# One stock of eight weight tiles in the FFN, and a shorter combination, in a two-layer attention, mLSTM and SwiGLU trunk

## The chip, the cores and the metric

The kernel runs on one core of one Trainium2 chip, as one launch. The metric is the device time of one execution in microseconds; the time before is the median of three runs. The engines are TensorE (PE; PEld where it loads weights), VectorE (DVE), ScalarE (ACT), GpSimd (POOL) and SyncE (SP), which issues nearly all loads.

## What is computed

Two layers on x of 256 rows and 2048 columns, all in float32. A layer normalizes, mixes (layer 0: sliding-window attention beside an mLSTM; layer 1: forgetting attention), adds, normalizes, and runs the FFN with 5632 hidden columns:

```python
def swiglu(xn, w_gate, w_up, w_down):
    return (jax.nn.silu(xn @ w_gate) * (xn @ w_up)) @ w_down

for layer in range(DEPTH):            # DEPTH = 2
    xn = rms_norm(h, norm_mix[layer])
    mix = swa_mlstm_mixer(...) if layer % 2 == 0 else forgetting_attention_mixer(...)
    h = h + mix
    h = h + swiglu(rms_norm(h, norm_ffn[layer]), w_gate[layer], w_up[layer], w_down[layer])
return rms_norm(h, norm_final)
```

## The kernel before

**Precision by splitting.** Every float32 operand of a large product is split in two: `hi`, cast by ScalarE to the reduced type float32r, and `lo`, the remainder, made by VectorE as the operand minus `hi`. A product is then three matmuls, hi by hi, hi by lo and lo by hi (`three`, L509 to L511, and the same in `gemm`, L212 to L214). x is kept as `xh`, `xl` and the input of the second product of each stage as `mh`, `ml`, both as 16 blocks of 128 rows (k) by 256 tokens; the tokens make two halves of 128, t0 and t1.

**Plain and mixed blocks.** `pair_group` multiplies by two weight matrices at once (gate and up; or two column blocks of w_down), 512 columns of each. It walks over pairs of k blocks in the order of `ORDER` (or `DOWN`): an entry (0, pair) is a plain block, (1, pair) a mixed one. A plain block loads 2 x 512 KB, splits both pieces and runs 2 x 2 x 2 x 3 = 24 matmuls into four PSUM banks, `plain`. A mixed block trades one product of eight for additions, in the manner of Strassen and Winograd: VectorE forms four sums of the two weight pieces (L568 to L571), these are split too (`ht`, `lt`), and they multiply sums of the x blocks that were formed once a layer (`sums_of`, kept in `sx`; for the down products in `sd`). It runs 21 matmuls, part into `plain` and part into four further banks, `prods`. At the end of the group `combine` (L523 to L530) forms from the four products the four corrections `c`, and these are added to `plain` (L619) before Silu (L621) and the product of gate and up (L623). A down group adds `c` and then `plain` into h (L708, L353).

**The FFN's course.** 11 groups of gate and up per layer, in parts of 3, 4 and 4 (`PARTS`). After each part its hidden columns are turned (by DMA transposes, or on TensorE after a last group) into `mh`, `ml`, and w_down's rows of that part are multiplied in two groups of 2 x 512 columns; the last half of the last layer uses `gemm` instead. The first FFN group takes over the turning of the second half of x: `todo` holds the joins that are due after the third and the fifth position (`LATER`), each of which splits a quarter of x and forms the sums of the mixed pairs 1, 3 and 5 in it.

**Tiles.** Weight pieces land in `raw` tiles, four in pool `wr` for plain blocks and four in the layer's pool `fp` for mixed ones. Their splits go to pool `wp`: tags `hi` and `lo`, six buffers each, taken in turn (L174, L175; for a mixed block also L565, L566). The two splits of a mixed block's sums go to tags `ht` and `lt` in `fp`, two buffers each (L578, L579). A tile is written again once the last matmul that reads it is done.

**What sets the order.** The program is written once, in the order of the Python code; a scheduler then lays the instructions of all engines out along its own timeline and fixes each engine's list. `issue_after` and the due times only steer it. Each engine runs its list in order and waits on counters of the other engines.

Of the kernel before, what the change touches and what calls it, by code (L numbers as in the profile page):

```python
# [24 lines left out]
CK = 2  # L25
# [10 lines left out]
ORDER = ((0, 0), (1, 1), (0, 2), (1, 3), (0, 4), (1, 5), (0, 6), (0, 7))  # L36
DOWN = {
# [35 lines left out]
def trunk(  # L73
# [26 lines left out]
    wp = ctx.enter_context(tc.tile_pool(name="wp", bufs=6))  # L100
# [72 lines left out]
    def split_chunk(raw, n):  # L173
        hi = wp.tile([P, CK, NB], F32R, tag="hi", name="hi")  # L174
        lo = wp.tile([P, CK, NB], F32R, tag="lo", name="lo")  # L175
        for k in (slice(0, 1), slice(1, CK)) if any(raw is f for f in fine) else (slice(0, CK),):
            latest[0] = nc.scalar.copy(hi[:, k, 0:n], raw[:, k, 0:n])  # L177
            nc.vector.tensor_tensor(  # L178
                out=lo[:, k, 0:n], in0=raw[:, k, 0:n], in1=hi[:, k, 0:n].bitcast(F32), op=ALU.subtract
            )  # L180
        return hi, lo
# [71 lines left out]
    def sums_of(pool, sh, sl, copies, full=None, tags=("tmp", "tmp"), bufs=None, box=None):  # L253
# [239 lines left out]
    def out_proj(w, idx, key, extra):  # L493
        last, rest = KT - 4, []
        for n0 in (0, 2):
# [3 lines left out]
            for i in range(2):  # L499
                gemm(accs[i], m_of, w, (n0 + i) * NB, NB, last, KT, KT, step=6)  # L500
                add_out(accs[i], n0 + i)
                (later if n0 == 0 else rest).append(
                    (LATER[n0 + i], split_turned(idx, n0 + i, *scrap(extra[2], n0 + i), extra))
                )
                square_sum(key, n0 + i)
        return rest

# [8 lines left out]
    def pair_group(fp, par, lhs, sums, mats, order, todo=(), halves=None, inner=None, raws=None):  # L516
        plain = [[bank(par, "acc") for _ in range(NT)] for _ in range(2)]
        todo = list(todo)
# [13 lines left out]
        for pos, (kind, pair) in enumerate(order):  # L532
# [4 lines left out]
            if not kind:  # L537
# [4 lines left out]
                for m, (w, c0) in enumerate(mats):  # L542
                    hi, lo = load_chunk(w, k0, c0, NB)
                    run_due(todo, pos)
                    for i, t in walk:
# [4 lines left out]
                            pos == 0 and i == 0, last and i == CK - 1,  # L550
# [14 lines left out]
            hu = wp.tile([P, CK, NB], F32R, tag="hi", name="hi")  # L565
            lu = wp.tile([P, CK, NB], F32R, tag="lo", name="lo")  # L566
# [6 lines left out]
            for src in (ra, rb) if halves else (t4, ra):  # L573
# [15 lines left out]
            three(plain[0][0], xb[:, t0], lb[:, t0], hg[:, 1, :], lg[:, 1, :], False, False)  # L589
            three(plain[1][0], sh[:, 3, :], sl[:, 3, :], hu[:, 1, :], lu[:, 1, :], False, False)  # L590
            three(prods[1], sh[:, 0, :], sl[:, 0, :], ht[0], lt[0], first, last)
            three(prods[2], sh[:, 2, :], sl[:, 2, :], ht[1], lt[1], first, last)
            three(prods[3], sh[:, 1, :], sl[:, 1, :], ht[2], lt[2], first, last)
            three(plain[0][1], xb[:, t1], lb[:, t1], ht[3], lt[3], False, False)
# [4 lines left out]
    def ffn(layer, fp, sx, sd, key, todo, idx_next=None, key_next=None, finish=None):  # L599
        r = rstd(key)  # L600

        def sums_x(pair):
            j = mixed_of(ORDER).index(pair)
            return sx[0][:, j, :, :], sx[1][:, j, :, :]

        for g0, g1 in zip(PARTS, PARTS[1:]):
# [3 lines left out]
            for g in range(g0, g1):  # L610
                par = (g1 - 1 - g) % 2
                plain, c = pair_group(
                    fp, par, x_of, sums_x, [(w_gate[layer], g * NB), (w_up[layer], g * NB)], ORDER, todo
                )
                todo = []
                for m in range(2):
                    for t in range(NT):
                        o = c[:, 2 * m + t, :]
                        nc.vector.tensor_tensor(out=o, in0=plain[m][t], in1=o, op=ALU.add)  # L619
                for t in range(NT):  # L620
                    nc.scalar.activation(c[:, t, :], c[:, t, :], AF.Silu, scale=r[:, t : t + 1])  # L621
                for t in range(NT):
                    nc.vector.scalar_tensor_tensor(  # L623
                        out=c[:, t, :], in0=c[:, 2 + t, :], scalar=r[:, t : t + 1], in1=c[:, t, :], op0=ALU.mult, op1=ALU.mult
# [47 lines left out]
            def sums_d(pair, order=order):  # L672
                j = mixed_of(order).index(pair)
                return sd[0][:, j, :, :], sd[1][:, j, :, :]
# [16 lines left out]
            for n0 in (0, 2):  # L691
# [13 lines left out]
                for m in range(2):  # L705
                    for t in range(NT):
                        o = h[:, t, (n0 + m) * NB : (n0 + m + 1) * NB]
                        nc.vector.tensor_tensor(out=o, in0=c[:, 2 * m + t, :], in1=o, op=ALU.add)  # L708
# [3 lines left out]
    def close_layer(layer, w_out, idx, key, **rest):  # L712
        with tc.tile_pool(name=f"fp{layer}", bufs=2) as fp:
# [3 lines left out]
            todo = out_proj(w_out, idx, key, (*sx, fp))  # L717
            sd = [fp.tile([P, nd, 4, P], F32R, tag=f"sd{i}", name=f"sd{i}", bufs=1) for i in range(2)]
            ffn(layer, fp, sx, sd, key, todo, **rest)
# [3 lines left out]
    hi = wp.tile([P, CK, NB], F32R, tag="hi", name="hi")  # L723
    lo = wp.tile([P, CK, NB], F32R, tag="lo", name="lo")
# [17 lines left out]
    with tc.tile_pool(name="ev", bufs=1) as ev:  # L742
# [223 lines left out]
        with tc.tile_pool(name="mp", bufs=1) as mp:  # L966
            def sums_m(pair):
                j = mixed_of(MIXQ).index(pair)
                return sx[0][:, j, :, :], sx[1][:, j, :, :]
# [129 lines left out]
    with tc.tile_pool(name="od", bufs=1) as od:  # L1099
# [65 lines left out]
        def sums_x(pair):  # L1165
            j = mixed_of(MIX).index(pair)
            return sx[0][:, j, :, :], sx[1][:, j, :, :]
# [154 lines left out]
```

## Time and profile before

| | us |
|---|---|
| median of three runs (lowest to highest) | 2077.54 (2077.33 to 2078.0) |
| span of the profiled execution | 2076.6 |
| TensorE busy (share of the span) | 2066.4 (100%) |
| VectorE busy | 1824.5 (88%) |
| ScalarE busy | 1374.7 (66%) |
| bytes read from HBM | 408.68 MB, 198 GB/s over the span |

The profiled execution's own time is its span; the median of the runs stands 0.9 us above it. A matmul's end in the profile is modelled and overlaps the start of the next, so a busy TensorE alone doesn't say that it runs at its full pace: the distance from start to start does. Busy times of VectorE and ScalarE are unions of overlapping instructions. The layout of the run: layer 0's mixer until about 323 us, its FFN until about 1010, layer 1's mixer until about 1380, its FFN until the end.

### The profile page before, as it was taken

To read this page: it belongs to the slowest core of one execution; us is meant where nothing else is said; L and a number is where in the kernel's file an instruction comes from. 1 tells how busy PE (TensorE), PEld (TensorE's weight loads), DVE (VectorE), ACT (ScalarE), POOL (GpSimd) and SP (SyncE) were. 2 spreads that over 40 slices of the span, in tenths; PEclk is the share of its full clock that TensorE was granted. 3 is DMA by queue.
4 is the path that set the end of the run, shared out by engine and by line. 5 is a ranking of instruction groups with operands and counts; after the bars stand their busy time and mean duration, and the time that the engine had idled before them with its cause. 6 is when DMAs were issued, how large, how long until landed. Compare 5 with 4: busy or idle time off the path is not lost.

```text
span 2076.6 us, 26994 instructions
## 1 busy us (share of the span) xinstructions
PE 2066.4 (100%) x9473; PEld 1715.0 (83%) x9473; DVE 1824.5 (88%) x2410; ACT 1374.7 (66%) x1736; POOL 41.7 (2%) x66
## 2 busy tenths in 40 slices
PE   9999999999999999999999999999999999999998
PEld 7878888888888888888888888888888888888887
DVE  6788769999999999999899778689999999999994
ACT  6777678765676656667676776687655667456763
POOL 1010000000000000000000001000000000000000
PEclk9999999999999999999999999999999999999999
DMA  8566577666566666666576866586665667666764
GB/s 292 172 213 188 190 247 236 203 217 206 189 230 223 205 210 205 220 212 204 185 215 204 235 193 184 156 283 220 206 205 200 213 206 234 203 202 213 220 197 138
DMA packets 309575, 434.87 MB, mean 209 GB/s; under 512 B 106412, under 2 KB 114624, under 8 KB 309312
## 3 DMA queue, kind: packets, MB, share of 16 engines
q1 hardware_dynamic: 307088, 426.27, 65.1%
q0 software_dynamic: 1632, 5.80, 0.8%
q8 instruction: 74, 1.21, 0.2%
q10 hardware_dynamic: 720, 1.09, 0.2%
q14 instruction: 61, 0.50, 0.1%
HBM read 408.68 MB, written 2.12 MB: 198 GB/s over the span
## 4 chain that ended last, share of the span: by engine, by line
PE 97%; DVE 1%; ACT 1%; DMA 1%; issue 1%; SPq 0%; POOLq 0%; POOL 0%; ACTq 0%; DVEq 0%
PE acc L510 21%; PE acc L509 21%; PE acc L511 21%; PE acc L213 5%; PE acc L212 5%; PE acc L214 5%; PE prod L509 5%; PE prod L510 5%; PE prod L511 5%; PE p L369 1%; PE po L470 1%; DMA raw<-in_w_in_odd_dram 0%; ACT s L403 0%; PE po L471 0%; DVE lo L178 0%
## 5 line engine op out<-in xcount | busy, mean ns | idle before, releaser
L177 ACT CAST hi<-raw 128x1024 fp32r<-128x1024 f32 (+3 forms) x656 | 664.8, 1028 | 440.2 <-PE acc L511 269.1
L178 DVE TENSOR_TENSOR lo<-raw,hi 128x1024 fp32r<-128x1024 f32 (+3 forms) x656 | 772.8, 1192 | 146.3 <-ACT hi L177 143.5
L510 PE MATMUL acc<-lo,xh 128*128 128x512 f32 x1254 | 488.6, 390 | 0.0
L509 PE MATMUL acc<-hi,xh 128*128 128x512 f32 x1254 | 485.9, 390 | 0.5 <-ACT hi L177 0.5
L511 PE MATMUL acc<-hi,xl 128*128 128x512 f32 x1254 | 484.8, 389 | 0.0
L510 PEld LDWEIGHTS acc<-lo,xh 128*128 128x128 f32 x1254 | 235.4, 188 | 49.4 <-DVE lo L178 0.6
L509 PEld LDWEIGHTS acc<-hi,xh 128*128 128x128 f32 x1254 | 235.2, 188 | 49.5 <-ACT hi L177 0.7
L511 PEld LDWEIGHTS acc<-hi,xl 128*128 128x128 f32 x1254 | 235.4, 188 | 48.8
L510 PE MATMUL acc<-lo,mh 128*128 128x512 f32 x437 | 169.7, 389 | 0.0
L511 PE MATMUL acc<-hi,ml 128*128 128x512 f32 x437 | 168.4, 389 | 0.0
L509 PE MATMUL acc<-hi,mh 128*128 128x512 f32 x437 | 167.9, 389 | 0.0
L339 ACT CAST hi<-raw 128x512 fp32r<-128x512 f32 x109 | 67.6, 620 | 89.4 <-PE acc L511 80.5
L213 PE MATMUL acc<-lo,mh 128*128 128x512 f32 (+1 forms) x322 | 126.3, 392 | 0.0
L212 PE MATMUL acc<-hi,mh 128*128 128x512 f32 (+1 forms) x322 | 125.8, 391 | 0.0
L214 PE MATMUL acc<-hi,ml 128*128 128x512 f32 (+1 forms) x322 | 123.7, 391 | 0.0
L340 DVE TENSOR_TENSOR lt<-t,ht 128x1024 fp32r<-128x1024 f32 x95 | 115.8, 1219 | 5.2 <-ACT ht L339 5.1
L339 ACT CAST ht<-t 128x1024 fp32r<-128x1024 f32 x95 | 99.9, 1051 | 30.7 <-PE prod L511 28.8
L339 ACT CAST ht<-raw 128x1024 fp32r<-128x1024 f32 x95 | 99.7, 1050 | 29.7 <-PE acc L511 15.0
L340 DVE TENSOR_TENSOR lt<-raw,ht 128x1024 fp32r<-128x1024 f32 x95 | 115.7, 1218 | 1.8 <-ACT ht L339 1.8
L213 PE MATMUL acc<-lo,xh 128*128 128x512 f32 (+3 forms) x288 | 99.8, 348 | 0.2 <-DVE lo L178 0.2
L214 PE MATMUL acc<-hi,xl 128*128 128x512 f32 (+3 forms) x288 | 98.1, 344 | 0.0
L212 PE MATMUL acc<-hi,xh 128*128 128x512 f32 (+3 forms) x288 | 95.9, 347 | 0.3
(363 smaller groups left out, 3448.0 us busy)
## 6 DMA issues: line engine op xcount, KB each, us to landing
raw<-in_w_gate_dram SPq DMA_DIRECT2D x176, 512.0 KB, 4.5
raw<-in_w_up_dram SPq DMA_DIRECT2D x176, 512.0 KB, 4.6
raw<-in_w_down_dram SPq DMA_DIRECT2D x176, 512.0 KB, 5.1
raw<-in_w_in_odd_dram SPq DMA_DIRECT2D x88, 512.0 KB, 4.9
raw<-in_w_in_even_dram SPq DMA_DIRECT2D x51, 512.0 KB, 5.0
raw<-in_w_out_even_dram SPq DMA_DIRECT2D x32, 512.0 KB, 5.1
raw<-in_w_out_odd_dram SPq DMA_DIRECT2D x32, 512.0 KB, 4.8
hr<-in_w_in_even_dram SPq DMA_DIRECT2D x12, 512.0 KB, 4.6
```

Source lines behind the costliest of these rows:

```text
L177: latest[0] = nc.scalar.copy(hi[:, k, 0:n], raw[:, k, 0:n])
L178: nc.vector.tensor_tensor(out=lo[:, k, 0:n], in0=raw[:, k, 0:n], in1=hi[:, k, 0:n].bitcast(F32), op=ALU.subtract)
L212: nc.tensor.matmul(o, ah[:, ts], hi, start=(k == 0), stop=False)
L213: nc.tensor.matmul(o, ah[:, ts], lo, start=False, stop=False)
L214: nc.tensor.matmul(o, al[:, ts], hi, start=False, stop=(k == k_all - 1 and cs.stop == n))
L339: nc.scalar.copy(dst_h, src)
L340: nc.vector.tensor_tensor(out=dst_l, in0=src, in1=dst_h.bitcast(F32), op=ALU.subtract)
L369: nc.tensor.matmul(pq[j % 2][:, j // 2, :], q_of(j, b), k_of(j)[:, 0:cols], start=True, stop=True)
L470: nc.tensor.matmul(po, v_of(j, 0), tt[:, j, 0:2, :].rearrange("p c q -> p (c q)"), start=True, stop=False)
L509: nc.tensor.matmul(o, ah, hi, start=start, stop=False)
L510: nc.tensor.matmul(o, ah, lo, start=False, stop=False)
L511: nc.tensor.matmul(o, al, hi, start=False, stop=stop)
```

## The change

The six slots of `wp` become a list of six pairs of fixed tiles, `weights`. `slot()` hands them out in turn, to plain blocks, to mixed blocks' raw pieces and, in the FFN, to the splits of their sums. In each layer's `close_layer` (output projection and FFN) two more pairs join the list and leave it at the end; they take the room of the `ht` and `lt` buffers in `fp`. In the mixers the splits of the sums go elsewhere (`halves`), as before. `combine`, where it belongs to the FFN, lays `c` out with the token half first and makes the last two adds one, whose first operand is one product read twice by a repeated access. The adds of `c` into h take 1024 columns at a time. `HEAVY` is an order with four mixed blocks; `DENSE`, the set of groups that would use it, is empty. The sums that the fourth pair (`FOURTH = 7`) would need are formed all the same: three of the four in places of `xh`, `xl` that ORDER leaves unread (`rooms`), the fourth in a new tile, `x4`. The scratch space of GpSimd's DMAs is halved from 4096 to 2048. `fresh` marks the first matmul into a bank; with ORDER it gives what the condition before it gave.

```diff
+HEAVY = ((1, 1), (0, 0), (1, 3), (0, 2), (1, 5), (0, 4), (1, 7), (0, 6))
+FOURTH = 7
+DENSE = ()
...
-    wp = ctx.enter_context(tc.tile_pool(name="wp", bufs=6))
+    wp = ctx.enter_context(tc.tile_pool(name="wp", bufs=1))
+    weights = [[wp.tile([P, CK, NB], F32R, name=f"{a}{i}") for a in ("hi", "lo")] for i in range(6)]
+
+    def slot():
+        weights.append(weights.pop(0))
+        return weights[-1]
...
     def split_chunk(raw, n):
-        hi = wp.tile([P, CK, NB], F32R, tag="hi", name="hi")
-        lo = wp.tile([P, CK, NB], F32R, tag="lo", name="lo")
+        hi, lo = slot()
...
-        split_plain(sh, sl, s)
+        if x4 is None:
+            split_plain(sh, sl, s)
+        else:
+            split_plain(sh, sl, s[:, 0:3, :])
+            split_plain(x4[:, 0, :], x4[:, 1, :], s[:, 3, :])
...
-            if extra is not None and pair in mixed_of(ORDER):
-                sh, sl, pool = extra
-                j = mixed_of(ORDER).index(pair)
+            if extra is not None and (pair in mixed_of(ORDER) or pair == FOURTH):
+                sh, sl, x4, pool = extra
...
-                sums_of(pool, sh[:, j, :, :], sl[:, j, :, :], copies)
+                if pair == FOURTH:
+                    sums_of(pool, rooms(xh), rooms(xl), copies, x4=x4)
+                else:
+                    j = mixed_of(ORDER).index(pair)
+                    sums_of(pool, sh[:, j, :, :], sl[:, j, :, :], copies)
...
+    def rooms(m):
+        return m[:, 2:11:4, P:S]
...
             c = fp.tile([P, 4, NB], F32, tag="c", name="c", bufs=1)
             nc.scalar.copy(c[:, 0, :], prods[0])
+            if halves is None:
+                nc.vector.tensor_tensor(out=c[:, 1, :], in0=prods[3], in1=c[:, 0, :], op=ALU.add)
+                nc.vector.tensor_tensor(out=c[:, 2, :], in0=prods[2], in1=c[:, 1, :], op=ALU.add)
+                nc.vector.tensor_tensor(
+                    out=c[:, 1:4:2, :],
+                    in0=prods[1].rearrange("p (a n) -> p a n", a=1).broadcast_to([P, 2, NB]),
+                    in1=c[:, 1:3, :],
+                    op=ALU.add,
+                )
+                return c
...
-            hu = wp.tile([P, CK, NB], F32R, tag="hi", name="hi")
-            lu = wp.tile([P, CK, NB], F32R, tag="lo", name="lo")
+            hu, lu = slot()
...
-                    hs = fp.tile([P, 2, NB], F32R, tag="ht", name="ht")
-                    ls = fp.tile([P, 2, NB], F32R, tag="lt", name="lt")
+                    hs, ls = slot()
...
-                for m in range(2):
-                    for t in range(NT):
-                        o = h[:, t, (n0 + m) * NB : (n0 + m + 1) * NB]
-                        nc.vector.tensor_tensor(out=o, in0=c[:, 2 * m + t, :], in1=o, op=ALU.add)
+                for t in range(NT):
+                    o = h[:, t, n0 * NB : (n0 + 2) * NB]
+                    nc.vector.tensor_tensor(
+                        out=o, in0=c[:, 2 * t : 2 * t + 2, :].rearrange("p a n -> p (a n)"), in1=o, op=ALU.add
+                    )
...
             sx = [fp.tile([P, nx, 4, P], F32R, name=f"sx{i}", bufs=1) for i in range(2)]
-            todo = out_proj(w_out, idx, key, (*sx, fp))
+            x4 = fp.tile([P, 2, P], F32R, name="x4", bufs=1)
+            more = [[fp.tile([P, CK, NB], F32R, name=f"{a}{i}", bufs=1) for a in ("hi", "lo")] for i in (6, 7)]
+            weights.extend(more)
+            todo = out_proj(w_out, idx, key, (*sx, x4, fp))
...
+            for pair in more:
+                weights.remove(pair)
...
-    nc = _bacc.Bacc("TRN2", target_bir_lowering=False, num_devices=1, dynamic_dma_scratch_size=4096)
+    nc = _bacc.Bacc("TRN2", target_bir_lowering=False, num_devices=1, dynamic_dma_scratch_size=2048)
```

More of the change, by code (lines that the diff above doesn't have):

```diff
@@ L251, in whole, with sums_of @@
         )
[L253 removed]
+    def sums_of(pool, sh, sl, copies, full=None, tags=("tmp", "tmp"), bufs=None, box=None, x4=None):
         if box is not None:
@@ L506, in out_proj, with four @@
         return rest
+    def four(s, j):
+        return [s[:, j, e, :] for e in range(4)]
+    def rooms(m):
+        return m[:, 2:11:4, P:S]
     def three(o, ah, al, hi, lo, start, stop):
@@ L517, in pair_group, with fresh @@
         plain = [[bank(par, "acc") for _ in range(NT)] for _ in range(2)]
+        begun = set()
+        def fresh(*at):
+            known = at in begun
+            begun.add(at)
+            return not known
         todo = list(todo)
@@ L588, in pair_group @@
             three(prods[0], xa[:, t0], la[:, t0], hg[:, 0, :], lg[:, 0, :], first, last)
[L589 to L594, printed above, removed]
+            three(plain[0][0], xb[:, t0], lb[:, t0], hg[:, 1, :], lg[:, 1, :], fresh(0, 0), False)
+            three(plain[1][0], sh[3], sl[3], hu[:, 1, :], lu[:, 1, :], fresh(1, 0), False)
+            three(prods[1], sh[0], sl[0], ht[0], lt[0], first, last)
+            three(prods[2], sh[2], sl[2], ht[1], lt[1], first, last)
+            three(prods[3], sh[1], sl[1], ht[2], lt[2], first, last)
+            three(plain[0][1], xb[:, t1], lb[:, t1], ht[3], lt[3], fresh(0, 1), False)
         if inner is None:
@@ L612, in ffn @@
                 plain, c = pair_group(
-                    fp, par, x_of, sums_x, [(w_gate[layer], g * NB), (w_up[layer], g * NB)], ORDER, todo
+                    fp,
+                    par,
+                    x_of,
+                    sums_x,
+                    [(w_gate[layer], g * NB), (w_up[layer], g * NB)],
+                    HEAVY if g in DENSE else ORDER,
+                    todo,
                 )
```

32 lines of the change are left out of this document (19 added, 13 removed).

## The prediction

> **What bounds the kernel now.** I read the page's head first, then TensorE's own list of waits, then the busy time by stretches of steady and unsteady stages, and last the timelines that show how far VectorE runs ahead of TensorE. The page of the kernel before:
>
> ```profile
> span 2076.6 us, 26994 instructions
> ...
> PE 2066.4 (100%) x9473; PEld 1715.0 (83%) x9473; DVE 1824.5 (88%) x2410; ACT 1374.7 (66%) x1736; POOL 41.7 (2%) x66
> ...
> PE 97%; DVE 1%; ACT 1%; DMA 1%; issue 1%; SPq 0%; POOLq 0%; POOL 0%; ACTq 0%; DVEq 0%
> ```
>
> TensorE is busy for 2066.4 of 2076.6 us and carries 97% of the chain. Its waits (total, times, longest, us) are these and no others:
>
> ```profile
> PE cold L159 <- POOL ones L156: 1.2, 1, 1.2
> PE acc L509 <- ACT hi L177: 0.5, 1, 0.5
> PE acc L213 <- DVE lo L178: 0.2, 1, 0.2
> ```
>
> 1.2 us lies before the first matmul. The other two, 0.7 us, are all that TensorE visibly lost to late operands in two layers. A modelled matmul end can hide a short slip, so the pace must be looked at too. Stretches, with busy time and count of PE, PEld, DVE, ACT, POOL, then clock and DMA:
>
> ```profile
> 323.00:364.30 41.30, 41.30 (x184) 34.21 (x183) 38.62 (x54) 35.95 (x50) 0.69 (x1) 1.00 0.74 228
> 841.10:882.60 41.50, 41.50 (x185) 34.35 (x183) 39.78 (x51) 28.36 (x32) 0.00 (x0) 1.00 0.66 216
> 1020.00:1120.00 100.00, 99.50 (x460) 82.74 (x459) 90.72 (x119) 69.98 (x83) 4.15 (x5) 1.00 0.74 230
> ```
>
> 841.10 to 882.60 is one gate/up group: five plain blocks of 24 matmuls and three mixed ones of 21, so 183, in 41.5 us: 0.227 us each, with VectorE 96% busy (39.78 of 41.5). Is 0.227 a wait for VectorE or TensorE's own pace? At the end of the program VectorE has stood idle for 9.93 us, and the pace is the same:
>
> ```profile
> 2062.13 0.39 PE L214 MATMUL acc<-hi,ml 128*128 128x512 f32 x1
> 2062.36 0.39 PE L212 MATMUL acc<-hi,mh 128*128 128x512 f32 x1
> 2062.58 0.39 PE L213 MATMUL acc<-lo,mh 128*128 128x512 f32 x1
> ...
> 2064.60 0.69 DVE L1244 TENSOR_TENSOR h<-acc,h 128x512 f32<-128x512 f32 x1 [9.93 <-PE acc L214]
> ```
>
> So the FFN already runs at TensorE's pace, and VectorE, nearly full, keeps up. Time can be gained only by fewer or shorter matmuls, and lost only where VectorE, ScalarE or a load comes late by more than its lead. How large the lead is, first in the tightest place (the first group of layer 0), then in a steady group:
>
> ```profile
> 338.43 0.28 DVE L264 TENSOR_TENSOR s<-full 128x128 f32<-128x128 f32 x1
> 338.63 0.28 DVE L262 TENSOR_TENSOR s<-full 128x128 f32<-128x128 f32 x1
> 338.86 1.23 DVE L340 TENSOR_TENSOR lt<-t,ht 128x1024 fp32r<-128x1024 f32 x1
> ...
> 341.34 0.69 DVE L568 TENSOR_TENSOR t<-raw 128x512 f32<-128x512 f32 x1
> 341.94 0.69 DVE L569 TENSOR_TENSOR t<-raw 128x512 f32<-128x512 f32 x1
> ...
> 342.75 1.22 DVE L178 TENSOR_TENSOR lo<-raw,hi 128x1024 fp32r<-128x1024 f32 x1
> 343.88 0.68 DVE L340 TENSOR_TENSOR lo<-raw,hi 128x512 fp32r<-128x512 f32 x1
> ...
> 824.10 1.22 DVE L340 TENSOR_TENSOR lt<-t,ht 128x1024 fp32r<-128x1024 f32 x1
> ```
> ```profile
> 342.63 0.39 PE L509 MATMUL prod<-ht,sx 128*128 128x512 f32 x1
> 342.86 0.39 PE L510 MATMUL prod<-lt,sx 128*128 128x512 f32 x1
> ...
> 829.33 0.39 PE L510 MATMUL prod<-lt,sx 128*128 128x512 f32 x1
> ```
>
> The remainder made at 338.86 ends at 340.09 and is first multiplied at 342.86: a lead of 2.77 us. The steady one ends at 825.32 and is used at 829.33: 4.01 us. The same rows give VectorE's true cost in a full queue, from start to start: 0.60 us for 512 columns (341.34 to 341.94), 1.13 for 1024 (342.75 to 343.88), 0.20 for 128 (338.43 to 338.63); the reported durations overlap.
>
> **The change part by part.** The instruction lists of the two builds hold the same 9,299 matmuls of the same shapes, the same 973 entries on SyncE's queue and the same 71 on GpSimd's; VectorE goes from 2,412 to 2,369 entries, ScalarE from 1,630 to 1,638. TensorE's floor is therefore unchanged, and each edit counts only by what it does to leads.
>
> *Combination (L526 to L529) and the adds into h (L708).* Each FFN block group takes three VectorE instructions where it took four, the last one of 1024 columns; each down group adds c into h in two of 1024 instead of four of 512.
>
> ```profile
> L621 ACT ACTIVATE c<-c,r 128x512 f32<-128x512 f32 x44 | 30.4, 718 | 3.5 <-DVE c L619 3.5
> L708 DVE TENSOR_TENSOR h<-c,h 128x512 f32<-128x512 f32 x44 | 29.5, 684 | 0.0
> L527 DVE TENSOR_TENSOR c<-prod,c 128x512 f32<-128x512 f32 x40 | 27.5, 688 | 0.8
> ```
>
> L621 runs twice per gate/up group: 22 groups. L708 runs four times per down group: 11. So 33 combinations lose one add, and 22 pairs of adds become 22 single ones (with the lost 33, the 55 fewer entries that the lists show before the 12 new ones). Each merge saves 2 x 0.60 - 1.13 = 0.07 us, 55 x 0.07 = 3.9 us of VectorE over the whole run, under 0.1 us for each group. All of it lies beside TensorE. No row shows a column read from PSUM twice by a repeated operand: at best it costs as 1024 columns (1.13), at worst it falls to a quarter of that pace (4.5); 3.4 us more in a group would then eat the steady lead of 4.0 but not pass it. I take 1.13, because L527, reading PSUM, lasts as long (688 ns) as L708 reading none (684). The banks that the products hold come free at the same point, 2 x 0.60 + 1.13 = 2.3 us after the first add, against 4 x 0.60 = 2.4.
>
> *The new sums of pair 7.* DENSE is empty, so no group uses them: they are pure extra, once a layer, when the last quarter of x is turned in the first FFN group. VectorE: four adds at 0.20, a split of 384 columns (about 0.47, between 0.20 and 0.60) and one of 128 (0.20): 1.5 us. ScalarE: two scaled copies and two casts, none wider than the 512 columns of L621's 0.72 us, so under 2.9 us; 41.3 - 35.95 = 5.4 us are free there. VectorE is 38.62 of 41.3 busy. If all 1.5 us falls ahead of one needed remainder, the lead goes from 2.77 to 1.3 us; no loss. Without that cover it would be 1.5 us a layer, 3.0 in all.
>
> *The stock of eight.* The plain blocks turned through six slots and the mixed blocks' sums through two of their own. Now a mixed block takes four of eight and a plain block two. The second pair of a mixed block needs what the previous mixed block's raw pieces held, free after 6 and 9 of its 21 matmuls instead of 15 and 21: 9 to 12 matmuls, 2.0 to 2.7 us earlier. The plain block after it waits as much longer, but it stands a whole mixed block ahead of TensorE (21 x 0.227 = 4.8 us), so nothing is late. Bounds: no gain where TensorE is full; a loss only past the leads of 2.8 to 4.0 us.
>
> *The order.* The scheduler lays all engines out anew: TensorE's list agrees for its first 758 matmuls and its last 246 and differs between. Alternations between the full-precision attention matmuls and the weight matmuls fall from 133 to 123, 10 fewer. No row quoted prices one; between nothing and one pitch of 0.227 each that is 0 to -2.3 us, and I take -0.4, nearer to nothing, since the unsteady stretch above (1020 to 1120) still shows TensorE busy for 99.5 of 100. The matmuls that carry a semaphore wait rise from 1,673 to 1,840; the one of 342.86, which waits for a remainder, follows the last at 0.23 like any other, so 0. What moves most is loads. At the change of layer the first large block of the odd layer was late:
>
> ```profile
> 1021.73 0.73 PE L509 MATMUL acc<-hi,xh 128*128 128x512 f32 x2 [0.47 <-ACT hi L177]
> ...
> 1023.33 1.05 ACT L177 CAST hi<-raw 128x1024 fp32r<-128x1024 f32 x1 [0.92 <-DMA raw<-in_w_in_odd_dram]
> ...
> 1024.63 1.05 ACT L177 CAST hi<-raw 128x1024 fp32r<-128x1024 f32 x1 [0.24 <-DMA raw<-in_w_in_odd_dram]
> ```
>
> In the new list that load is issued 23 small matmuls earlier and used 18 later, behind one large and two small loads more. Two casts in a row that waited for their loads start 1.3 us apart (1023.33, 1024.63), so a large load adds 1.3 us to the queue and a small one, 272 columns of 512, 0.7: 2.7 us later against 18 + 23 matmuls at 0.125, 5.1 us. I take the loss of 0.5 us as gone. Against that, in the first down projection of each layer one load now stands 20 matmuls (4.5 us) ahead of its use where the closest was 55. It needs
>
> ```profile
> raw<-in_w_down_dram SPq DMA_DIRECT2D x176, 512.0 KB, 5.1
> ```
>
> 5.1 and a cast of 1.05, so 6.2 us, and 7.4 with the remainder. But the chip's leads are longer than the list's: 7 matmuls (1.6 us) stood between the remainder of 338.86 and its use, counted from its start, and the chip showed 4.0 from start to use; 8 (1.8 us) for that of 824.10, and 5.2. Adding these 2.4 to 3.4 us gives 6.9 to 7.9 us: enough for the cast, short by at most 0.5 for the remainder. Two layers: 0 to 1.0 us, taken as 0.5.
>
> **Sum.** Against the profiled 2076.6 us: matmuls 0, VectorE 0, alternations -0.4, layer change -0.5, late load +0.5: 2076.2. The median of the runs, 2077.54, stands 0.9 above that span; so 2077.1 us, no change that this kernel's measurement can tell (0.2% is 4.2 us).
>
> The Trainium skill, page "Perfetto Trace Analysis", section "Identifying the Most-Contended Engine", holds that matmul occupancy says little about headroom and that the share of weight loading does. By it the 83% of PEld would leave 17% of TensorE free, and a deeper stock could use it; the equal pace beside an idle VectorE speaks against that.
>
> **The rivals.** *Faster, because the pace is not the floor.* Then 0.227 hides waits, the weight load's 1715.0 / 9473 = 0.181 us would be the bound, and the eight slots would let TensorE pull ahead. Price: if even a twentieth of 0.046 us on some 8,500 matmuls went, 20 us, 2057. The idle end of VectorE with the same pace is against it. Chance 3%, the other gains over 4.2 us included.
>
> *Slower, by late operands in the first FFN part.* Place: group 1 to the first down projection of each layer. If the chip had no longer leads there than the list, the load of 20 matmuls comes 7.4 - 4.5 = 2.9 us late and the unused sums push 1.5 us before it: 4.4 us a layer, 8.8 in all, 2086. It decides once the two layers lose more than 2.1 us each. For it: VectorE has only 41.3 - 38.62 = 2.7 us free there. Against: the leads measured. Chance 15%.
>
> The Trainium skill, page "TensorE: Matmul & The Clock Gate", Part 1, says that an idle window of about 3.4 us halves the PE clock, which would make such a hole dearer; no stretch here is idle that long, and the clock reads 1.00.
>
> *The change does not do what it says:* the stock is deeper, but nothing waited for it; that is my forecast, 82%.
>
> **How the numbers follow.** No change has 82%, its own range 2075.0 to 2080.0: down by all the alternations (-2.3, in place of -0.4), up by a late load of 1.0, the hole kept and up to 2 us of the slow case's kind. To leave out under 2 in 10, the range goes into the slow case: 2074.5 to 2082.0. Faster by over 0.2% 0.03, within 0.82, slower 0.15.
>
> **What would show it.** Right: PE busy again within 2 us of 2066, its waits under 2 us in all, VectorE about 1 us less loaded (3.9 saved, 3.0 new), a steady group still 41.5 us. The hole at 1021 gone. Wrong: PE rows waiting for L177's or L178's successors between 440 and 520 or 1500 and 1580 us; the combined add far over 1.22 us; or a pace under 0.227.

## The result, and the profile after

The changed kernel takes 2104.66 us (median of four runs, 2103.56 to 2104.97) against 2077.77 us for the kernel before on the same chip (2077.33 to 2078.06): a ratio of 1.0129 with a 95% interval of 1.0115 to 1.0143. It is slower by 27 us, and the forecast, 2077.1 in a range up to 2082.0, was wrong.

The head of the page and the chain that ended last, of the changed kernel:

```profile
span 2102.8 us, 26924 instructions
...
PE 2072.5 (99%) x9473; PEld 1718.5 (82%) x9473; DVE 1821.5 (87%) x2367; ACT 1373.8 (65%) x1744; POOL 41.4 (2%) x66
...
PE 94%; ACT 2%; DVE 2%; DMA 1%; issue 1%; SPq 1%; POOLq 0%; POOL 0%; ACTq 0%; DVEq 0%
```

TensorE was idle for 10 us of the span before; now it is idle for 30 us, and busy 6 us longer with the same 9,473 instructions. Its list of waits (total, times, longest, us) says where the idle time is:

```profile
PE pp L471 <- DVE s L431: 9.5, 1, 9.5
PE acc L220 <- ACT mh L359: 7.3, 1, 7.3
PE acc L530 <- ACT hi L185: 1.3, 2, 0.7
...
PE pom L1089 <- DVE st L1093: 0.8, 1, 0.8
PE pom L1089 <- DVE hv L1097: 0.7, 1, 0.7
```

Two single waits, the first two rows, hold 16.8 us. Neither is in the feed-forward part, where the prediction had looked for late operands. The one for `s` is at 1317 us, in layer 1, and the one for `mh` at 247 us, in layer 0; each time the last attention block (the last mLSTM head in layer 0) ends there and the output projection (`out_proj`, lines L220 to L222) has begun.

The stages say the same. The last matmul of layer 0's output projection starts at 334.5 us (before: 322.7), the last of its feed-forward part at 1022.0 (1009.3), the last of layer 1's output projection at 1405.5 (1380.5). So the two mixers with their output projections take 11.8 and 12.3 us longer, and the two feed-forward parts 0.9 and 1.2: together the 26.2 us between the spans. The busy time by stretches (length, then PE, PEld, DVE, ACT, POOL with their counts, then granted clock, DMA share, GB/s), of the changed kernel:

```profile
247.00:255.00 8.00, 0.70 (x4) 0.30 (x2) 2.01 (x8) 3.35 (x8) 0.28 (x1) 0.60 0.23 52
255.00:259.00 4.00, 4.00 (x10) 3.14 (x11) 2.19 (x7) 2.69 (x8) 0.69 (x1) 0.52 0.48 115
1316.00:1328.00 12.00, 2.47 (x11) 1.64 (x9) 7.36 (x15) 5.45 (x18) 0.00 (x0) 0.68 0.43 131
1328.00:1334.00 6.00, 6.00 (x22) 5.09 (x22) 1.83 (x6) 1.17 (x2) 0.00 (x0) 0.50 0.00 0
854.80:896.20 41.40, 41.40 (x185) 34.28 (x184) 40.12 (x51) 28.29 (x32) 0.00 (x0) 1.00 0.70 216
```

and the same two stages in the kernel before:

```profile
240.00:250.00 10.00, 10.00 (x46) 8.35 (x45) 7.48 (x20) 6.00 (x16) 1.42 (x2) 1.00 0.26 73
1310.00:1320.00 10.00, 10.00 (x51) 8.34 (x50) 6.79 (x13) 6.83 (x20) 0.00 (x0) 1.00 0.51 159
```

Before, TensorE was full there. Now it stands still for most of 247 to 255 and 1316 to 1328, and after each hole it runs at a granted clock (the share of its full clock that TensorE is given) of about a half (0.52 and 0.50). The last row of the changed kernel is a steady gate/up group: 41.4 us, as before (41.5). The steady feed-forward part has lost nothing.

What filled the place before? TensorE's timeline of the kernel before, from the scores of the last attention block (L369) to the transposes of its weights (L456):

```profile
1301.68 1.91 PE L369 MATMUL p<-ktf,qtf 128*128 128x128 f32 x10
1303.24 0.58 PE L213 MATMUL acc<-lo,mh 128*128 128x512 f32 x1
1303.66 0.40 PE L214 MATMUL acc<-hi,ml 128*128 128x512 f32 x1
...
1318.18 0.39 PE L212 MATMUL acc<-hi,mh 128*128 128x512 f32 x1
1318.41 0.27 PE L456 MATMUL pp<-ident,s 128*128 128x128 f32 x1
```

and of the changed kernel, with its new line numbers (L384, L220 to L222, L471):

```profile
1316.16 1.03 PE L384 MATMUL p<-ktf,qtf 128*128 128x256 f32 x4
1316.84 0.58 PE L222 MATMUL acc<-hi,ml 128*128 128x512 f32 x1
1317.25 0.39 PE L220 MATMUL acc<-hi,mh 128*128 128x512 f32 x1
1317.48 0.40 PE L221 MATMUL acc<-lo,mh 128*128 128x512 f32 x1
1317.72 0.40 PE L222 MATMUL acc<-hi,ml 128*128 128x512 f32 x1
1327.64 1.45 PE L471 MATMUL pp<-ident,s 128*128 128x128 f32 x4 [9.53 <-DVE s L431]
```

The softmax between scores and transposes runs on VectorE and ScalarE. Before, 66 matmuls of the output projection, 15 us, stood between the two on TensorE; now 4. So the transposes stand at the head of TensorE's queue and wait 9.53 us. The filler has not vanished: it comes after the attention instead of beside it.

### The profile page after: what moved, and what is told of

The parts are those of the page before. It is cut to its first block, busy times and chain, and to the rows that moved or that the text cites. A ratio compares the mean times of both kernels' runs of the same rounds, so it can differ in the third digit from the quotient of the medians.

```text
span 2102.8 us, 26924 instructions
## 1 busy us (share of the span) xinstructions
PE 2072.5 (99%) x9473; PEld 1718.5 (82%) x9473; DVE 1821.5 (87%) x2367; ACT 1373.8 (65%) x1744; POOL 41.4 (2%) x66
## 4 chain that ended last, share of the span: by engine, by line
PE 94%; ACT 2%; DVE 2%; DMA 1%; issue 1%; SPq 1%; POOLq 0%; POOL 0%; ACTq 0%; DVEq 0%
PE acc L530 20%; PE acc L531 20%; PE acc L532 20%; PE acc L221 5%; PE acc L220 5%; PE acc L222 5%; PE prod L530 5%; PE prod L532 5%; PE prod L531 5%; DVE lo L186 1%; PE p L384 1%; PE po L485 1%; ACT hi L185 1%; ACT s L418 0%; DMA raw<-in_w_out_odd_dram 0%
## 5 line engine op out<-in xcount | busy, mean ns | idle before, releaser
L531 PE MATMUL acc<-lo,xh 128*128 128x512 f32 x1320 | 513.9, 389 | 0.0
L532 PE MATMUL acc<-hi,xl 128*128 128x512 f32 x1320 | 511.2, 389 | 0.0
L530 PE MATMUL acc<-hi,xh 128*128 128x512 f32 x1320 | 506.2, 390 | 0.0
L354 ACT CAST hi<-raw 128x512 fp32r<-128x512 f32 x204 | 166.9, 819 | 159.5 <-PE acc L532 80.7
L355 DVE TENSOR_TENSOR lo<-raw,hi 128x512 fp32r<-128x512 f32 x204 | 190.2, 932 | 14.0 <-ACT hi L354 12.8
L354 ACT CAST hi<-t 128x1024 fp32r<-128x1024 f32 x95 | 100.0, 1053 | 68.6 <-PE acc L532 40.7
L220 PE MATMUL acc<-hi,mh 128*128 128x512 f32 (+1 forms) x322 | 125.4, 393 | 7.8 <-ACT mh L359 7.3
L355 DVE TENSOR_TENSOR lo<-t,hi 128x1024 fp32r<-128x1024 f32 x95 | 115.7, 1218 | 16.1 <-ACT hi L354 15.8
L222 PE MATMUL acc<-hi,ml 128*128 128x512 f32 (+1 forms) x322 | 124.5, 392 | 0.0
L530 PEld LDWEIGHTS acc<-hi,mh 128*128 128x128 f32 x466 | 87.3, 188 | 20.2 <-ACT hi L185 2.2
L532 PEld LDWEIGHTS acc<-hi,ml 128*128 128x128 f32 x466 | 87.5, 188 | 18.2
L531 PEld LDWEIGHTS acc<-lo,mh 128*128 128x128 f32 x466 | 87.5, 188 | 18.2
```

The source lines that it names most:

```text
L220: nc.tensor.matmul(o, ah[:, ts], hi, start=(k == 0), stop=False)
L222: nc.tensor.matmul(o, al[:, ts], hi, start=False, stop=(k == k_all - 1 and cs.stop == n))
L354: nc.scalar.copy(dst_h, src)
L355: nc.vector.tensor_tensor(out=dst_l, in0=src, in1=dst_h.bitcast(F32), op=ALU.subtract)
L530: nc.tensor.matmul(o, ah, hi, start=start, stop=False)
L531: nc.tensor.matmul(o, ah, lo, start=False, stop=False)
```

## The experiments

**The theories.** The stock of weight tiles is handed out in turn, and the changed kernel lets the two extra pairs join it (`weights.extend(more)`) before the output projection is written down. *Theory A, memory:* the extra pairs lie in the feed-forward pool, on addresses that the mixer's tiles still hold; when the turn comes to them, the next weight block of the output projection can't be written until the last attention is through, and everything behind it waits too. *Theory B:* another part of the change, the merged adds, the unused sums of pair 7 or the new order of the feed-forward part, is the cause. *Theory C, depth:* with eight pairs the output projection simply runs further ahead and has been used up when the attention needs cover.

**The join moved behind the output projection.**

```
-            weights.extend(more)
             todo = out_proj(w_out, idx, key, (*sx, x4, fp))
+            weights.extend(more)
```

> The two extra pairs of slots lie where they lay in the changed kernel, but join the stock only after the output projection of each layer has been written down; everything else of the change stays. Theory A (memory: the extra pairs lie on tiles that the last attention of the layer still uses, so the stock, which is handed out in turn, stops at them in the middle of the output projection): 2076 to 2081 us, TensorE's two holes of 7 to 10 us near 247 and 1317 us gone, the waits of 0.7 and 0.9 us in the first down projections still there. Theory B (the combination, the unused sums of pair 7 or the FFN's new order): nothing of these is touched, so 2100 us or more and both holes. Theory C (depth: with eight pairs the output projection runs too early and is then missing as filler beside the last attention): as A, since its depth is six again; this run does not tell A from C.

Measured: 2081.48 us against 2076.99, ratio 1.0020 (1.0011 to 1.0029). Both holes are gone; the stretches of this kernel:

```profile
247.00:255.00 8.00, 8.00 (x37) 6.62 (x37) 3.56 (x13) 4.23 (x13) 0.59 (x1) 1.00 0.23 52
1316.00:1328.00 12.00, 12.00 (x65) 10.27 (x64) 8.08 (x12) 5.76 (x8) 0.00 (x0) 1.00 0.55 174
```

Theory B falls for the holes: one moved line takes back 22.9 of the 26.2 us between the profiled spans (2102.8, 2079.9 and 2076.6). Some 3 to 4.5 us stay (3.3 by these spans, 4.5 by the medians); the median lies half a microsecond above the range expected by theory A.

**Six pairs, two of them in the feed-forward pool.** During the output projection only:

```
             weights.extend(more)
+            away = [weights.pop(0) for _ in range(2)]
             todo = out_proj(w_out, idx, key, (*sx, x4, fp))
+            weights.extend(away)
```

> The changed kernel, but during the output projection two of the six old pairs are set aside, so that it turns through six: four old ones and the two in the memory that the last attention still uses. Theory A (memory): the turn reaches the blocked pairs just the same and has only four free ones before them, so 2100 us or more, holes at both places, each at least 7 us. Theory C (depth): six pairs, as in the kernel before, so 2076 to 2082 us without the holes. Theory B: as the changed kernel, 2104.

Measured: 2104.19 us, 1.0128 (1.0113 to 1.0144), as slow as the whole change at the old depth of six. Theory C, which asked for no holes here, falls. The waits are not where theory A put them, though:

```profile
PE ptv L1132 <- DVE hv L1105: 8.6, 2, 4.9
PE acc L220 <- ACT hi L185: 3.3, 3, 1.6
PE prod L531 <- DVE lo L355: 2.4, 4, 1.2
```

In layer 1, 34 weight matmuls now stand between scores and transposes, and the wait there is 0.8 us, where A had asked for 7. By stages, as above, layer 0's mixer with its output projection takes 13.4 us more than before, layer 1's 5.5 and the two feed-forward parts 8.1 together. So the total agrees with that of the changed kernel by chance; what speaks against C is the loss beside the output projections at a depth of six. Why the feed-forward parts lose more here was not tried.

**Early in layer 0 only.**

```
-            weights.extend(more)
+            if layer == 0:
+                weights.extend(more)
             todo = out_proj(w_out, idx, key, (*sx, x4, fp))
+            if layer == 1:
+                weights.extend(more)
```

> The extra pairs join before the output projection in layer 0, as in the changed kernel, and after it in layer 1. Theories A and C: half of the loss goes: the hole near 247 us stays at 7 to 8 us with its half clock behind it, the one near 1317 us is gone, 2088 to 2094 us. Theory B: 2104.

Measured: 2093.54 us, 1.0075 (1.0061 to 1.0089). The hole of layer 0 stays (6.4 us for L220), that of layer 1 is gone. The two layers lose alike, about 11 to 12 us each.

**The extra pairs at other addresses.**

```
             x4 = fp.tile([P, 2, P], F32R, name="x4", bufs=1)
+            fp.tile([P, CK, NB], F32, tag="raw", name="raw", bufs=RAWS)
+            fp.tile([P, 96], F32, name="pad", bufs=1)
             more = ...
```

> The extra pairs join where the changed kernel lets them join, with eight pairs in the output projection, but they lie 16.8 KB further up in the same pool. In layer 1 that is the memory of the mixer's raw weight loads, which are done before the last attention; in layer 0 it is memory of tiles that the last attention still uses. Theory A (memory): the hole near 1317 us goes, the one near 247 stays: 2088 to 2095 us. Theory C (depth): eight pairs are eight pairs wherever they lie: both holes stay, 2100 us or more. Theory B: 2104.

Measured: 2117.39 us, 1.0191 (1.0177 to 1.0205). Both holes stay (9.7 and 7.3 us), so theory A, as it stood, failed here, though the run with six pairs had ruled out C. The order of instructions in the build shows why: the first write into the extra pair waits, in this kernel as in the changed one, for the same long list:

```
first cast into hi6, layer 1, waits for: its own load, and the last instructions of
  VectorE and ScalarE on the last attention's transposed weights (tt), of GpSimd on its
  mask (cb0), and five of GpSimd's transfers for the mixer (cb1, scratch)
first cast into hi6, layer 0, waits for: the last instructions of VectorE and ScalarE on the
  last mLSTM head's output (hv, st), and five of GpSimd's transfers for the mixer (nat, ends,
  edge_b, rows)
```

The transposed weights lie below the moved pairs, and the list is the same at both places: it does not depend on the address. **Theory A2:** the first write into any tile of a new pool waits until the work on the pool that was there before is done, whatever the tile's address; it is a wait that the program is built with, not one that the chip adds. The extra pairs are the first tiles of the feed-forward pool that anything writes, long before the pool is needed for itself.

**The extra pairs lent by the raw loads.** In layer 1 the four tiles come from a pool of their own that stays open; during the mixer they take its raw loads and are given back tile by tile:

```
+    rp = rp_ctx.enter_context(tc.tile_pool(name="rp", bufs=1))
+    raws1 = [rp.tile([P, CK, NB], F32, tag=f"{a}{i}", name="raw", bufs=1) for i in (6, 7) for a in ("hi", "lo")]
...
-            more = [[fp.tile([P, CK, NB], F32R, name=f"{a}{i}", bufs=1) ...
+            more = [[(lent or fp).tile([P, CK, NB], F32R, tag=f"{a}{i}", name=f"{a}{i}", bufs=1) ...
```

> Eight pairs in the output projection, joined as early as in the changed kernel, but in layer 1 the two extra pairs are cut from tiles of a pool of their own, which during the mixer hold its raw weight loads and are given back one by one when the last mixed block has read them; layer 0 is as in the changed kernel. Theory A2 (whole pool: the first write into the feed-forward pool waits until every engine has done with the mixer's pool, whatever the address): layer 1's wait goes, since these tiles are not in that pool; its hole near 1317 us is gone, the one near 247 us stays: 2090 to 2096 us, as when only layer 0 joins early. Theory C (depth): eight pairs are eight, the hole near 1317 us stays, 2102 us or more.

Measured: 2093.25 us, 1.0076 (1.0061 to 1.0091), as when only layer 0 joins early. With eight pairs in its output projection layer 1 has no hole, and 61 weight matmuls stand beside the softmax; layer 0, left as it was, has its own:

```profile
244.00:260.00 16.00, 7.67 (x22) 5.48 (x23) 8.12 (x27) 9.47 (x25) 1.44 (x3) 0.70 0.35 99
1300.00:1330.00 30.00, 30.00 (x151) 25.49 (x150) 20.85 (x25) 19.23 (x34) 1.37 (x1) 1.00 0.72 232
```

In this build the first cast into `hi6` of layer 1 waits for its own load alone. A2 holds for layer 1: which pool the pairs belong to decides, not how many there are and not where they lie. For layer 0 the same remedy was not tried; there the list of waits in the build and the late join, which takes the hole away, speak for A2.

**The merged adds alone**, in the kernel before:

```
+            if halves is None:
+                (three adds, the last of 1024 columns; indices 2 * t + m as in the change)
...
-                        nc.vector.tensor_tensor(out=o, in0=c[:, 2 * m + t, :], in1=o, op=ALU.add)
+                        out=o, in0=c[:, 2 * t : 2 * t + 2, :].rearrange("p a n -> p (a n)"), in1=o, op=ALU.add
```

> The kernel before with one part of the change: the combination in three adds instead of four and the adds into the residual in two instead of four; stock, sums and order of tiles as before. If this part costs nothing, as predicted: within 2 us of the kernel before, 2075 to 2079. If the column read twice from PSUM by a repeated operand is slow, or the products' banks come free later: 2080 us or more, and the late join explains only the rest.

Measured: 2079.29 us against 2077.59, 1.0007 (0.9998 to 1.0016): no change that can be told, though the median lies 0.3 us above the expected range and the trace has one new wait, at the change of layer (1011 us), where layer 1's first transposes of h wait for the add into h:

```profile
PE pt L275 <- DVE h L353: 1.7, 1, 1.7
```

**The late join without the sums of pair 7.**

```
-            if extra is not None and (pair in mixed_of(ORDER) or pair == FOURTH):
+            if extra is not None and pair in mixed_of(ORDER):
```

> The late join in both layers, without the unused sums of pair 7. The late join alone stands at 2081.5 against 2077.0 us. If the unused sums are what is left of the loss: 2076 to 2078.5 us. If the stock of eight in the feed-forward part costs it: 2080.5 to 2083 us.

Measured: 2081.24 us, 1.0018 (1.0010 to 1.0027). With the sums the ratio was 1.0020: they cost nothing that can be seen, and what is left of the loss, some 4 us, is not theirs.

**Layer 0 late, layer 1 lent, no sums.** The edits of the runs above together.

> Layer 0 joins late, layer 1 early with the tiles lent by the raw loads, and no unused sums. Theory A2: no hole of more than 2 us in TensorE anywhere, 2075 to 2081 us; under 2076 only if eight pairs in an output projection gain something over six. Theory C: a hole of 7 to 10 us near 1317 us, 2088 us or more.

Measured: 2080.39 us, 1.0015 (1.0006 to 1.0024). No hole over 1 us is left after the start, and eight pairs in an output projection gain nothing that can be told over six.

**The stock of eight alone**, joined early, with the old adds and no new sums.

> Only the stock of eight, joined before the output projection as in the changed kernel; the combination, the adds into the residual and the sums as in the kernel before. Theory A2 (the first write into the feed-forward pool waits for the whole of the mixer's pool): all of the large loss is here: 2099 to 2104 us, holes of 7 to 10 us near 247 and 1317 us. If the combination or the sums have a share in the holes: under 2096 us.

Measured: 2107.58 us, 1.0146 (1.0132 to 1.0160), with both holes:

```profile
PE pp L471 <- DVE s L431: 10.5, 1, 10.5
PE acc L220 <- ACT mh L359: 7.1, 1, 7.1
```

The stock is enough to make the loss; without the merged adds and the sums it is even over 3 us above my upper bound.

**The stock of eight alone, joined late.**

> Only the stock of eight, joined after the output projection. The late join of the whole change stands 4 us above the kernel before, the combination alone 1.7 above it, the sums at 0.2. If these small costs add up: 2079 to 2081 us here. If the stock in the feed-forward part is free and the combination is what costs: 2077 to 2078.5.

Measured: 2084.75 us, 1.0035 (1.0021 to 1.0049), above both expectations. In the feed-forward part and around it the stock of eight costs 7 us by itself, in small waits (none over 1.5 us by this list):

```profile
PE prod L531 <- DVE lo L355: 1.7, 2, 1.5
PE acc L530 <- ACT hi L185: 1.3, 2, 1.0
...
PE acc L531 <- DVE lo L186: 1.0, 2, 0.8
```

With the merged adds it was 1.0018 (1.0010 to 1.0027). So they seem to win back about half of it, though the two intervals overlap. In the profiled runs the difference lies in layer 0's feed-forward part, which takes 5.2 us more than before without the merged adds and 0.4 with them.

**One extra pair instead of two.**

```
-            more = [[... for a in ("hi", "lo")] for i in (6, 7)]
+            more = [[... for a in ("hi", "lo")] for i in (6,)]
```

> The changed kernel with one extra pair instead of two, so a stock of seven, joined before the output projection. Theory A2: the turn stops at the first pair of the new pool, so one stops it as two do: 2098 us or more, both holes of at least 6 us. If the loss goes with the amount of memory taken: about half, 2089 to 2094 us.

Measured: 2110.97 us, 1.0159 (1.0145 to 1.0173). The two holes are 7.0 us each; a stock of seven adds waits of its own in the feed-forward part (3.5 us for `mh` in the first down projections). The loss does not go with the amount of memory: one pair of the new pool in the turn stops the turn.

**Using the sums: a fourth mixed block in six groups**, on top of the late join.

```
-DENSE = ()
+DENSE = (3, 6, 9)
```

> The late join, and a fourth mixed block in three gate/up groups of each layer (the groups 3, 6 and 9), which uses the sums of pair 7: three matmuls fewer in each of six groups, 18 of 0.227 us, so 4.1 us of TensorE. VectorE makes 6.4 us of work for a mixed block against 2.3 for a plain one (estimated from 1.13 us for 1024 columns and 0.60 for 512), 4.1 us more in a group with 1.7 us free: if its lead of 4 us carries that and is won back in the plain groups, 2076.5 to 2078.5 us; if not, each of the six groups loses up to 2.4 us on TensorE, 2081 to 2092 us.

Measured: 2087.88 us, 1.0049 (1.0036 to 1.0062), with 18 matmuls fewer and yet some 6 us more than the late join alone: the second of the two cases. VectorE is 22.5 us busier (1843.6 against 1821.1). The largest waits:

```profile
PE prod L530 <- DVE xl L360: 2.9, 1, 2.9
PE acc L530 <- ACT hi L185: 2.4, 2, 1.2
```

They lie not in the six groups but in the down projections (at 991, 674 and 1740 us). The two feed-forward parts take 4.3 us longer than with the late join alone, with 4.1 us less of matmuls. That VectorE's free time doesn't carry the fourth block is argued from its load, not shown. No version here beats the kernel before.

## Why the prediction was wrong, point by point

**The step that failed is "The stock of eight".** It said: "nothing is late. Bounds: no gain where TensorE is full; a loss only past the leads of 2.8 to 4.0 us." It followed the eight pairs through mixed and plain blocks of the feed-forward part alone. It did not ask who else takes pairs from the stock, nor when the new pairs can first be written. The output projection takes them too, and the new pairs belong to a pool whose first write waits for the end of the mixer. How many weight matmuls stand between scores and transposes of layer 1's last attention, in the order of the build, tells the kernels with a hole in that layer from those without:

```
                               weight matmuls   wait at the transposes, us
before                               66            none listed
join after the projection            59            none listed
lent by the raw loads                61            none listed
six, two in the new pool             34            0.8
changed                               4            9.5
other addresses                       4            9.7
stock alone                           4           10.5
one extra pair                        4            7.0
```

**The size of it.** The early join costs 22.9 us (2102.8 against 2079.9). The two long waits are 16.8, two short ones just ahead of the first hole 1.5 (L1089, 0.8 and 0.7). The rest is the half clock. After the hole of layer 0 the changed kernel's matmuls start 0.43 us apart, until 258.84:

```profile
254.85 0.79 PE L220 MATMUL acc<-hi,mh 128*128 128x512 f32 x1 [7.30 <-ACT mh L359]
255.44 0.63 PE L221 MATMUL acc<-lo,mh 128*128 128x512 f32 x1
255.87 0.63 PE L220 MATMUL acc<-hi,mh 128*128 128x512 f32 x1
...
258.84 0.39 PE L221 MATMUL acc<-lo,mh 128*128 128x512 f32 x1
```

Nine of them take 3.99 us, from 254.85 to 258.84, instead of 9 x 0.227 = 2.04: 1.9 us lost. In layer 1 the half pace lasts from 1327.64 to about 1334.0, so half of 6.4 us: 3.2. Together 16.8 + 1.5 + 1.9 + 3.2 = 23.4, within 0.5 of the 22.9. The two terms of the half clock, 5.1 us, agree with TensorE's busy time, which is 4.9 us longer than with the late join (2072.5 against 2067.6) for the same matmuls.

**"The order" failed with it, in its sign.** The fall from 133 to 123 alternations between attention matmuls and weight matmuls was priced as a gain of 0.4 us. Counted by place, the stretch around layer 0's last mLSTM heads falls from 26 to 16 and that around layer 1's last attention from 18 to 10. The alternations that went were the cover itself; with the late join there are 135. The list had shown the loss, and I had read only its total.

**What held.** TensorE's floor and the steady group: 41.4 us against 41.5. The combined add: predicted at the price of 1024 columns,

```profile
L557 DVE TENSOR_TENSOR c<-prod,c 128x1024 f32<-128x1024 f32 x33 | 40.1, 1214 | 0.0
```

1214 ns, so the column read twice costs nothing extra. The sums of pair 7 are hidden (1.0020 with them and 1.0018 without in the two late joins; VectorE's busy time is 4.3 us shorter without, which TensorE doesn't feel). The hole at the layer change is gone: TensorE is busy for all of the 100 us from 1020, where it was for 99.5.

The late load in the first down projections, given 0 to 1.0 us for both layers and taken as 0.5, was too small: it shows 1.3 us in two waits, at 483 and 1554 us, the places that the prediction had named as its sign of being wrong. ScalarE's cast, for which TensorE waits, had waited 1.3 and 1.5 us for the load. The first, in layer 0:

```profile
483.01 0.74 PE L530 MATMUL acc<-hi,mh 128*128 128x512 f32 x2 [0.58 <-ACT hi L185]
```

**What was mis-sized besides.** The stock was put at nothing; joined late, it costs 3.7 us with the merged adds (1.0018) and 7 us without (1.0035), and the adds, costed as hidden, are then worth some 3 us. I expected the leads to absorb all of it. The waits are scattered (0.2 to 1.5 us, at about 262, 265, 471 and 1283 us among others). Those at 262, 265 and 1283 lie in the output projection, which with the late join turns through six pairs as before, so they don't come from the longer turn itself; for the others, the longer turn and the new order were not separated. The late join alone, with a median of 2081.48 us, would have been just inside the range.

**The rivals.** The slower one had its place wrong: it put 8.8 us into the stretch from group 1 to the first down projection, where the waits are 0.6 and 0.7 us, and where the whole feed-forward parts lost 0.9 and 1.2. That a hole would be dearer through the clock was right. The Trainium skill, page "TensorE: Matmul & The Clock Gate", Part 1, has the clock fall to half after an idle window of about 3.4 us and rise again after about as long at work. The trace shows the fall and the rise, but not after these times: the clock fell 1.0 and 2.3 us into the two waits, and the half pace lasted 4.0 and 6.4 us after them. The last section has more of both. The faster rival is out: the pace of 0.227 us is the same with eight pairs.

## What to carry to other kernels

When a tile joins a rotating stock, follow the turn through every user of the stock, and look at the first write into the tile: here, where it belonged to a pool that had just opened, it waited for the work on the pool before it, and so did all that was handed out behind it. Where a latency chain (a softmax, a normalisation with its transposes) is covered by filler matmuls, count the filler in the built order, place by place, before and after: a total of alternations that falls can be cover that has gone. A hole of 7 to 10 us in TensorE cost its length and some 2 to 3 us more at half clock here.

## What the runs showed of the hardware

The half clock after a hole did not last equally long: 4.0 us after 7.3 us of waiting, when large matmuls of 512 columns followed at once, and 6.4 us after 9.5 us, when small transposes and products of 128 and 256 columns followed. The size of the matmuls is not the reason. In the run with one extra pair the same small ones follow layer 1's hole (7.0 us, until 1329.05), and the half pace ends 3.4 us later. Stretches cut where the granted clock changes, of the changed kernel (layer 0, then layer 1):

```profile
255.40:258.80 3.40, 3.40 (x9) 2.64 (x8) 1.60 (x5) 2.11 (x6) 0.69 (x1) 0.50 0.44 100
258.82:262.00 3.18, 3.18 (x17) 2.63 (x16) 2.56 (x5) 3.02 (x8) 0.00 (x0) 1.00 0.21 79
1327.20:1334.00 6.80, 6.36 (x22) 5.27 (x23) 2.62 (x9) 1.17 (x2) 0.00 (x0) 0.50 0.00 0
1334.02:1338.00 3.98, 3.98 (x21) 3.38 (x21) 2.73 (x4) 3.08 (x4) 0.00 (x0) 1.00 0.00 0
```

and of the run with one extra pair (layer 1):

```profile
1325.70:1332.40 6.70, 3.35 (x13) 2.89 (x14) 2.29 (x10) 3.60 (x14) 0.00 (x0) 0.50 0.21 74
1332.50:1335.00 2.50, 2.50 (x17) 2.18 (x15) 0.54 (x2) 0.70 (x2) 0.00 (x0) 1.00 0.00 0
```

By the traces' records of the granted clock, it stands at a half from 248.57 to 258.81 and from 1320.36 to 1334.01 in the changed kernel, and from 1325.63 to 1332.45 with one extra pair: 10.24, 13.65 and 6.83 us, which are three, four and two steps of 3.41. Each time the full clock returns at the end of the first step that TensorE worked through without a wait. In the changed kernel TensorE began again 0.55 us before the end of a step in layer 0 and 2.96 us before it in layer 1, and needed one whole step more: 0.55 + 3.41 = 4.0 and 2.96 + 3.41 = 6.4. With one extra pair it began at the start of a step: 3.4.

Nor does the clock need a long hole to fall. In the run with six pairs it was halved for one such step, from 1337.78 to 1341.19, after waits of no more than 1.6 and 0.5 us close together; in the step before, TensorE was busy for about half of the time:

```profile
1334.40:1337.70 3.30, 1.70 (x6) 1.12 (x7) 2.94 (x3) 1.97 (x3) 0.00 (x0) 1.00 0.00 0
1337.80:1341.10 3.30, 3.30 (x9) 2.62 (x8) 0.01 (x1) 0.53 (x1) 0.00 (x0) 0.50 0.86 290
```

At other addresses the same feed-forward matmuls ran a little slower. In the run with the extra pairs further up, one line's matmuls, first in the changed kernel:

```profile
L531 PE MATMUL acc<-lo,xh 128*128 128x512 f32 x1320 | 513.9, 389 | 0.0
```

and then in that run:

```profile
L531 PE MATMUL acc<-lo,xh 128*128 128x512 f32 x1320 | 515.5, 391 | 0.0
```

and a steady gate/up group of that run, by its stretch:

```profile
859.00:900.80 41.80, 41.80 (x185) 34.27 (x184) 39.84 (x50) 28.38 (x33) 0.00 (x0) 1.00 0.69 214
```

A steady group takes 41.8 us against 41.4, at full clock and with no wait listed, and that run is 12.7 us above the changed kernel with holes of the same size; by stages, 11.7 us of it lie in the two feed-forward parts. Raw tiles and the tiles behind them moved as well as the extra pairs, so which operand's place matters stays open.
